# Weight sums of the down projection made from DRAM to DRAM, and two more gate/up pairs by Strassen's scheme, in a two-layer fp32 decoder trunk on one core

## Chip, core, metric

The kernel runs on one core of one Trainium2 chip. The metric is the device time of one execution, in microseconds (us), as a median of several. Where a time is taken from one profiled execution, the text says so.

The engines that matter: TensorE (PE: matmuls, with its weight loads shown as PEld), VectorE (DVE), ScalarE (ACT), GpSimd (POOL) and the 16 DMA engines of the core, which are fed by three queues: one that SyncE (SP) issues, one that ACT issues and one that POOL issues. In the profile these are q1 (SP), q10 (ACT) and q0 (POOL).

## What is computed

Two layers on x of 512 tokens by 1024 features, in fp32. Each layer has a mixer (layer 0: causal pooling; layer 1: causal differential attention), then a SwiGLU feed-forward with 2816 hidden features:

```python
x = layernorm(ALPHA * x + mixer(x))
x = layernorm(ALPHA * x + (silu(x @ w_gate) * (x @ w_up)) @ w_down)
```

The change is in the feed-forward of both layers. Every fp32 product is made of three fast matmuls: each operand is split into a high part (ACT rounds it, a CAST in the profile) and a low part (DVE subtracts the high part), and high·high, high·low and low·high are summed.

## The kernel before

**Weights.** A list `wall` in DRAM holds all weights in blocks of 128x1024 fp32 (512 KB). SP loads blocks in order into five `raw` buffers (`RAWS`, `refill`). ACT and DVE split a block into a pair of parts, six of which fit (`WBUFS`).

**Gate and up products (`ffn`).** The 22 columns of 128 hidden features form 11 pairs; pair k holds columns k and k+11. A pair needs four blocks. An ordinary pair (`plain`, called for each column f) makes four products of 24 matmuls with 512 moving columns. A pair in `SPLIT` (`strassen(k)`) splits the 2x2 block product of {gate, up} x {first, second half of the features} x {first, second 256 tokens} by Strassen's scheme: seven products P1, Q5, P6, Q3, P7, P2, Q4 of 24 matmuls with 256 moving columns. It pays for this with sums: four sums of two weight blocks on DVE (L566, in place in the raw buffers), sums of quarters of x, made once per layer into `xs` (`sums_of_x`: twelve DVE operations of 128x1024 and four ACT casts), and DVE and ACT operations that combine the products (L829 to L849). Before, pairs 4 to 10 are split and pairs 0 to 3 are ordinary. At the start of a layer the first columns (three in layer 0, two in layer 1) are done in halves of 256 tokens, since x arrives late.

**Order.** The program is written out by hand, and each engine keeps its own order. After each product `ahead` issues the splits for later products, so that parts are ready about five products early. An engine goes on as soon as its own queue and semaphores let it; nothing else ties a queue to the place where an instruction stands in the code.

**Down projection.** It uses the same scheme with seven products, over items (p, i): p one of the seven, i one of six groups of rows of `w_down` (`PAIRS`: five of two rows, one of one). Three of the seven take blocks of `wall` as they are; the other four take sums of blocks: with b0 to b3 the four blocks of a group, b0+b1, b1+b3, b0+b1+b3 and b0+b1+b3+b2. Before, they are made during the gate and up products of the same layer, in eleven slices: `load_terms` has POOL issue two loads of 512 KB into free rows of `hid` or into the buffer `gb`, and a third that adds to the first as it lands (`accum_op`); `sum_terms` has DVE make two sums of 128x512 (L671, L672), and then ACT issue two stores to `tsum` in DRAM. The down phase reads `tsum` back through SP (`fetch_item`).

**Affine.** The LayerNorm gain and bias that belong to the residual (`affine(n, s)`: two DVE operations of 128x1024 per 128 tokens, L205 and L206) are done early in each gate phase. The parameters sit in `gb`.

**POOL** also raises the variance to the power -1/2 for each LayerNorm (L177), makes one low part per attention head (`sql`, L110), and issues loads of `ssum` in the down phase (L726).

Of the kernel before, what the change touches and what calls it, by code (L numbers as in the profile page):

```python
# [12 lines left out]
F32 = mybir.dt.float32  # L13
# [3 lines left out]
ALU = mybir.AluOpType  # L17

P = 128
# [3 lines left out]
DEPTH = 2  # L23
# [31 lines left out]
def trunk(ctx, tc, x, wall, pscale, lam_p, subln, table, lng, lnb, band, first, onehot, out):  # L55
# [398 lines left out]

# [8 lines left out]
    def ffn(layer, late):  # L463
# [5 lines left out]
        with tc.tile_pool(name=f"ffn{layer}", bufs=1) as fp:  # L469
# [6 lines left out]


            order = [k + j * HALF for k in range(HALF) for j in range(2)]
            tsum = dram.tile([4, len(PAIRS), P, 1024], F32, name=f"tsum{layer}")
            ssum = dram.tile([P, 2, 2, HALF, 256], F32, name=f"ssum{layer}")  # L480

            def block(i, b):

                if PAIRS[i][1] == 2:
                    return wall[c1 + 4 * i + b]
                return wall[c1 + 20 + b // 2][:, (b % 2) * 512 : (b % 2 + 1) * 512]


            items = [(p, i) for p in DOWN for i in range(len(PAIRS))]
# [4 lines left out]
            def fetch_item(j):  # L494
                p, i = items[j]
                w = 512 * PAIRS[i][1]
                t = keep.tile([P, 1024], F32, tag="raw", name=f"r{layer}_{j}", bufs=RAWS)[:, :w]
                src = {"P1": 0, "P2": 2, "Q3": 3}
                if p in src:
                    nc.sync.dma_start(out=t, in_=block(i, src[p]))  # L500
# [78 lines left out]
            def ahead(upto):  # L579
                advance(upto)  # L580
                if upto > len(chunks):
                    prepare(upto - len(chunks), upto - len(chunks))

            def product(acc, j, lo, hi):
                h, l = halves[j]
                for k in range(KB):
                    mm3(
                        wide(acc, lo, hi),
                        (h[:, k * P : (k + 1) * P], l[:, k * P : (k + 1) * P]),
                        x_at(k, lo, hi),  # L590
                        k == 0,
                        k == KB - 1,
                    )
# [47 lines left out]
                low(3, r3)  # L641
                yield

            terms = {}
            rows_of = hid.rearrange("p (j k) t -> p j k t", j=2)

            def term_slice(k):
                return slice(k % 2 * 512, (k % 2 + 1) * 512)  # L650

            def load_terms(k):
                if k < HALF - 1:
                    c = c1 + 4 * (k // 2)
                    src = wall[c : c + 4][:, :, term_slice(k)].rearrange("(j r) p t -> p j r t", j=2)
                else:
                    src = wall[c1 + 20 : c1 + 22].rearrange("j p (r t) -> p j r t", r=2)
                if k == 1:
                    t = rows_of[:, :, 4:6, :]
                elif k % 2 == 0 and k < HALF - 1:  # L660
                    t = rows_of[:, :, 9:11, :]
                else:
                    t = keep.tile([P, 2, 2, 512], F32, tag="gb", name=f"b{layer}_{k}")
                for j in range(2):
                    nc.gpsimd.dma_start(out=t[:, j], in_=src[:, j])  # L665
                nc.gpsimd.dma_start(out=t[:, 0], in_=src[:, :, 1], accum_op=ALU.add)  # L666
                terms[k] = t

            def sum_terms(k):
                t = terms.pop(k)  # L670
                tt(t[:, 1, 1], t[:, 0, 0], t[:, 1, 1], op=ALU.add)  # L671
                tt(t[:, 1, 0], t[:, 1, 1], t[:, 1, 0], op=ALU.add)  # L672
                yield
                dst = tsum[:, k // 2, :, term_slice(k)].rearrange("(j r) p t -> p j r t", j=2)
                for j in range(2):
                    nc.scalar.dma_start(out=dst[:, j], in_=t[:, j])
                if k + 2 < HALF - 1 and k != 1:
                    load_terms(k + 2)
                if k == HALF - 2:
                    load_terms(HALF - 1)  # L680

            summed_rows = [0]
            behind = []

            def weight_sums():
                g = sum_terms(summed_rows[0])
                summed_rows[0] += 1
                next(g)
                behind.append(g)

            def sum_hidden(k):

# [45 lines left out]
            def prepare(upto, lefts):  # L738
# [11 lines left out]
            load_terms(0)  # L750
            load_terms(1)
            sums = sums_of_x()
            for lo in (0, 256):
                for f in range(early):
                    for i in range(2):
                        product(accs[f][i], 2 * f + i, lo, lo + 256)
                        if not lo and (f, i) in late:
                            late[f, i]()
                        if not lo:
                            advance(2 * early, True)  # L760
                    if lo:
                        advance(2 * f + 6)
                        gated(order[f], *accs[f])
                        affine(n - 1, f)
                        catch_up()
                        if f < 2:
                            weight_sums()
                            next(sums)
                        if f == 1:
                            behind.append(sum_hidden(0))  # L770

            def plain(f):
                k = f // 2
                j = index[k] + 2 * (f % 2)
                a = (bank(f"g{layer}_{f}"), bank(f"u{layer}_{f}"))
                for i in range(2):
                    product(a[i], j + i, 0, S)
                    ahead(j + i + 5)
                    if f >= 3:
                        next(sums, None)  # L780
                    catch_up()
                gated(order[f], *a)
                if f < SB:
                    affine(n - 1, f)
                if f in (3, 5, 7):
                    weight_sums()
                if f == 3:
                    load_terms(3)
                if f % 2:
                    behind.append(sum_hidden(k))  # L790

            def strassen(k):
# [18 lines left out]
                for j, p in enumerate(GATE):  # L811
# [15 lines left out]
                    if p == "P1":  # L827
                        g0 = tile_of(0)
                        nc.scalar.copy(both(g0), acc)  # L829
                    elif p == "Q5":  # L830
                        nc.scalar.copy(second, acc)  # L831
                    elif p == "P6":
                        nc.scalar.copy(first, acc)
                    elif p == "Q3":
                        tt(first, acc, first, op=ALU.subtract)  # L835
                    elif p == "P7":
                        tt(second, second, acc, op=ALU.subtract)
                    elif p == "P2":
                        tt(both(g0), acc, both(g0), op=ALU.add)  # L839
                    else:  # L840
                        g1 = tile_of(1)
                        nc.scalar.activation(both(g1), acc, AF.Silu)
                    ahead(index[k] + j + 6)
                    catch_up()
# [5 lines left out]
                if k < HALF - 1:  # L850
                    weight_sums()
                behind.append(sum_hidden(k))

            f = early
            while f < FB:
                if f // 2 in SPLIT:
                    strassen(f // 2)
                    f += 2
                else:
                    plain(f)  # L860
                    f += 1
            load_gb(n)

            while behind:
# [90 lines left out]
    def attention(late):  # L955
        n = 2
        with tc.tile_pool(name="attn", bufs=1) as ap:
# [225 lines left out]
            for h in range(HEADS):  # L1183
# [35 lines left out]
                ready(where[0] + 3)  # L1219
                if h > 0:  # L1220
                    mix(h - 1)
                start_scores(h)
                score_block(h, 0)
                score_block(h, 1)
# [152 lines left out]
```

## Time and profile before

| | |
|---|---|
| median of 3 runs | 951.18 us (951.01 to 952.31) |
| profiled execution | 951.38 us |
| its span, first to last instruction | 949.6 us |
| mean granted TensorE clock | 0.997 |

The profiled execution lies 0.20 us above the median, and 1.78 us of it are outside the span. The stages, in us from the span's start: pooling mixer to about 44; gate and up of layer 0 to 269, with the Strassen pairs from 127.85; down of layer 0 to 367; attention to about 600; gate and up of layer 1 to 836, with the Strassen pairs from 695.00; down and the last LayerNorm to the end.

How to read the rows: in the chain and the timeline a row has start, duration, engine, line and what it writes from what; "x24" is a number of instructions merged; in brackets stand the idle time ahead of a row and what ended it. In rows by window the columns are the window, its length, then busy time of PE, PEld, DVE, ACT, POOL (number of instructions in brackets), the granted clock, the mean busy share of the 16 DMA engines, and GB/s. Instructions of one engine overlap a little: two sums of 128x1024 take 2.48 together, where one alone takes 1.22. A DMA row gives the size and the median time from issue to landing.

### The profile page before, as it was taken

The page shows a single profiled execution, that of the slowest core. Times are in us where ns is not written, and L with a number is a line of the kernel's source. Part 1 is how long each engine was busy: PE and PEld are TensorE (multiplying, and loading weights), DVE is VectorE, ACT ScalarE, POOL GpSimd, SP SyncE. Part 2 cuts the span into 40 slices and gives each one's busy share as a digit, 9 for nine tenths or more (in the row PEclk, how much of TensorE's full clock was granted, in tenths as well). Part 3 has the DMA queues.
Part 4 walks back from the last instruction along what each step waited for, and adds up shares of the span by engine and source line. Part 5 has one row for each costly group of instructions (what it writes and reads, how often), then busy time and mean ns, then how long its engine had stood idle before and what let it go on. Part 6 is the DMA issues. An engine that isn't in the chain of part 4 may idle for free.

```text
span 949.6 us, 15363 instructions
## 1 busy us (share of the span) xinstructions
PE 934.6 (98%) x5976; PEld 845.9 (89%) x5976; DVE 783.4 (82%) x1149; ACT 489.9 (52%) x788; POOL 108.6 (11%) x133
## 2 busy tenths in 40 slices
PE   9899999999999999999999999999999999999996
PEld 8798899999988888988888888998899999988885
DVE  8858989999988688688777677789779999987678
ACT  6662245555554467665556552833344554564450
POOL 4120211110001200000000000211111110001101
PEclk9999999999999999999999999999999999999998
DMA  9288998976878964323242233396978885878942
GB/s 237 100 261 256 302 290 265 268 237 212 263 249 272 361 221 133 115 89 100 60 141 79 67 89 89 109 319 191 295 254 248 249 269 205 260 247 275 352 175 90
DMA packets 82248, 196.99 MB, mean 207 GB/s; under 512 B 14804, under 2 KB 26324, under 8 KB 82174
## 3 DMA queue, kind: packets, MB, share of 16 engines
q1 hardware_dynamic: 42876, 115.07, 37.1%
q0 software_dynamic: 15520, 46.14, 17.7%
q10 hardware_dynamic: 23778, 34.78, 10.1%
q8 instruction: 47, 0.77, 0.3%
q14 instruction: 27, 0.22, 0.1%
HBM read 159.25 MB, written 36.72 MB: 206 GB/s over the span
## 4 chain that ended last, share of the span: by engine, by line
PE 90%; DVE 6%; ACT 2%; issue 1%; DMA 1%; POOL 0%; DVEq 0%; SPq 0%; POOLq 0%
PE A L820 17%; PE P L886 13%; PE C L820 8%; PE Q L886 6%; PE B L820 4%; PE g L129 3%; PE u L129 3%; PE u L128 3%; PE u L127 3%; PE g L128 3%; PE g L127 3%; PE s L1085 2%; PE v L127 2%; PE v L129 2%; PE v L128 2%; PE q L128 2%
## 5 line engine op out<-in xcount | busy, mean ns | idle before, releaser
L566 DVE TENSOR_TENSOR raw<-raw,raw 128x1024 f32<-128x1024 f32 x56 | 68.3, 1219 | 0.5
L224 ACT ACTIVATE y<-pt,bT,gT 128x128 f32<-128x128 f32 x96 | 36.0, 455 | 22.7 <-PE pt L213 22.7
L109 ACT CAST xs<-hid 128x512 fp32r<-128x512 f32 (+1 forms) x60 | 34.7, 581 | 24.4 <-DVE hid L734 24.4
L110 DVE TENSOR_TENSOR xs<-hid,xs 128x512 fp32r<-128x512 f32 (+1 forms) x60 | 38.4, 642 | 7.8 <-ACT xs L109 7.8
L1095 ACT ACTIVATE p<-p,mn 128x128 f32<-128x128 f32 (+3 forms) x64 | 35.3, 553 | 14.9 <-DVE mn L1090 14.9
L665 POOL DMA_DIRECT2D b<-in_wall x20 | 14.0, 707 | 175.6 <-DMA tsum<-b 92.6
L726 POOL DMA_DIRECT2D xs<-ssum x24 | 17.4, 727 | 141.5 <-PE Q L886 120.3
L598 DVE TENSOR_TENSOR hid<-sg,u 128x512 f32<-128x512 f32 x16 | 11.0, 687 | 26.1 <-PE u L129 14.1
L177 POOL TENSOR_TENSOR rs<-rs,mhalf 128x1 f32<-128x1 f32 x16 | 12.5, 784 | 172.2 <-DVE rs L176 132.8
L110 DVE TENSOR_TENSOR xt<-y,xt 128x512 fp32r<-128x512 f32 x24 | 16.3, 689 | 17.4 <-ACT xt L109 17.4
L665 POOL DMA_DIRECT2D hid<-in_wall x24 | 18.7, 822 | 84.5 <-DMA tsum<-hid 30.7
L1090 DVE CUSTOM_DVE_ANT_0 p<-s,bias 128x128 f32<-128x128 f32 (+3 forms) x64 | 28.1, 485 | 0.0
L110 POOL TENSOR_TENSOR sql<-sq,sqh 128x512 fp32r<-128x512 f32 x7 | 9.1, 1293 | 165.3 <-ACT sqh L109 165.3
L702 ACT CAST v<-u 128x512 fp32r<-128x512 f32 x22 | 13.6, 620 | 26.9 <-DVE u L700 26.7
L168 DVE BATCH_NORM_STATS2 st<-res 128x6 f32<-128x512 f32 x32 | 22.2, 695 | 1.1
L846 ACT ACTIVATE sg<-sg 128x512 f32<-128x512 f32 x14 | 8.9, 633 | 25.7 <-DVE sg L839 25.7
L110 DVE TENSOR_TENSOR heads<-k,heads 128x512 fp32r<-128x512 f32 x8 | 5.5, 693 | 19.9 <-ACT heads L109 19.9
L614 ACT CAST xs<-hid 128x1024 fp32r<-128x1024 f32 x8 | 8.4, 1051 | 24.1 <-DVE hid L631 11.6
L666 POOL DMA_DIRECT2D hid<-in_wall x12 | 14.8, 1232 | 50.1 <-DMA hid<-in_wall 50.1
L1109 DVE SCALAR_TENSOR_TENSOR p<-p,sm,p 128x128 f32<-128x128 f32 (+3 forms) x32 | 17.6, 551 | 1.1
L835 DVE TENSOR_TENSOR hid<-C,hid 128x512 f32<-128x512 f32 x14 | 9.7, 691 | 10.4 <-PE C L820 8.8
L831 ACT COPY hid<-C 128x512 f32<-128x512 f32 x14 | 8.2, 587 | 19.4 <-PE C L820 19.4
(1119 smaller groups left out, 3726.3 us busy)
## 6 DMA issues: line engine op xcount, KB each, us to landing
raw<-in_wall SPq DMA_DIRECT2D x122, 512.0 KB, 4.6
r<-tsum SPq DMA_DIRECT2D x40, 512.0 KB, 4.3
hid<-in_wall POOLq DMA_DIRECT2D x36, 512.0 KB, 7.1
b<-in_wall POOLq DMA_DIRECT2D x30, 512.0 KB, 5.7
r<-in_wall SPq DMA_DIRECT2D x30, 512.0 KB, 4.9
tsum<-hid ACTq DMA_DIRECT2D x24, 512.0 KB, 5.3
ssum<-v ACTq DMA_DIRECT2D x22, 512.0 KB, 4.1
tsum<-b ACTq DMA_DIRECT2D x20, 512.0 KB, 5.1
```

What stands on the lines that cost most here:

```text
L109: nc.scalar.copy(dst_h, src)
L110: (low or nc.vector).tensor_tensor(dst_l, src, dst_h.bitcast(F32), op=ALU.subtract)
L127: nc.tensor.matmul(acc, ah, bh, start=start, stop=False)
L128: nc.tensor.matmul(acc, ah, bl, start=False, stop=False)
L129: nc.tensor.matmul(acc, al, bh, start=False, stop=stop)
L224: nc.scalar.activation(y[:, k, :], pt[:, k * P : (k + 1) * P], AF.Identity, bias=bT[:, n, kk : kk + 1], scale=gT[:, n, kk : kk + 1],)
L566: tt(t, raws[pair[0]], raws[pair[1]], op=ALU.add)
L665: nc.gpsimd.dma_start(out=t[:, j], in_=src[:, j])
L820: nc.tensor.matmul(o, w[:, c], x[:, kk, :], start=p in ("P1", "Q5", "P2") and f + kk + e == 0, stop=p in ("Q4", "Q3", "P2") and (f, kk, e) ...
L886: nc.tensor.matmul(accs[s], x[:, k, r], y[:, c], start=first and k == 0 and e == 0, stop=last and k == m - 1 and e == 2, skip_group_check= ...
L1090: nc.vector.tensor_tensor_reduce(out=p, in0=accs[c][:, :w], in1=biases[h][:, w - 1 :: -1] if w < S else biases[h][:, ::-1], op0=ALU.add, o ...
L1095: nc.scalar.activation(p, p, AF.Exp, bias=mn[:, q, c : c + 1], scale=-1.0, accum_out=sm[:, q, c : c + 1],)
```

## The change

- The four sums of down-weight blocks are made from DRAM to DRAM, with no buffer in SBUF and nothing on DVE or ACT: for each, six copies of block or earlier sum into `sums[layer][q][i]`, then six DMAs that add another block to it as they land. All 48 per layer are issued by POOL, with at most 8192 B per descriptor row. `load_terms`, `sum_terms`, `weight_sums` and `tsum` go.
- The code takes these steps from a generator: for layer 0, `pace()` after each gate or up product takes 0.69 step on average; for layer 1, six steps stand in each of the eight attention heads.
- `SPLIT` gains pairs 2 and 3, in both layers. The layout of `wall` follows.
- `sums_of_x` starts as soon as x is complete and is done before pair 2.
- The affine operations move from the first columns to the Strassen pairs 3 to 10: one DVE operation at each Q3 (`affines`).

```diff
-SPLIT = (4, 5, 6, 7, 8, 9, 10)
+SPLIT = (2, 3, 4, 5, 6, 7, 8, 9, 10)
...
+    sums = [
+        [
+            [
+                dram.tile([P, 512 * m], F32, name=f"t{layer}_{q}_{i}")
+                for i, (_, m) in enumerate(PAIRS)
+            ]
+            for q in range(4)
+        ]
+        for layer in range(DEPTH)
+    ]
...
+    def sum_steps(layer, c):
+
+        made = sums[layer]
+        for q, start, b in ((0, None, 1), (1, None, 3), (3, 0, 3), (2, 3, 2)):
+            for adds in range(2):
+                for i in range(len(PAIRS)):
+                    if adds:
+                        source, op = block(c, i, b), dict(accum_op=ALU.add)
+                    else:
+                        source, op = made[start][i] if start is not None else block(c, i, q), {}
+                    nc.gpsimd.dma_start(
+                        out=made[q][i], in_=source, max_dma_last_dim=8192, **op
+                    )
+                    yield
...
                 else:
                     m = {"Q5": 0, "P6": 3, "P7": 1, "Q4": 2}[p]
-                    nc.sync.dma_start(out=t, in_=tsum[m, i, :, :w])
+                    nc.sync.dma_start(out=t, in_=sums[layer][m][i])
...
-            def load_terms(k):
...
-                for j in range(2):
-                    nc.gpsimd.dma_start(out=t[:, j], in_=src[:, j])
-                nc.gpsimd.dma_start(out=t[:, 0], in_=src[:, :, 1], accum_op=ALU.add)
-                terms[k] = t
-
-            def sum_terms(k):
-                t = terms.pop(k)
-                tt(t[:, 1, 1], t[:, 0, 0], t[:, 1, 1], op=ALU.add)
-                tt(t[:, 1, 0], t[:, 1, 1], t[:, 1, 0], op=ALU.add)
-                yield
...
-                for j in range(2):
-                    nc.scalar.dma_start(out=dst[:, j], in_=t[:, j])
...
+            def affines():
+                for s in range(SB):
+                    for j, op in enumerate((ALU.mult, ALU.add)):
+                        tt(res[:, s, :], res[:, s, :], gbs[n - 1][:, j, :], op=op)
+                        yield
...
+            xsums, scaling = sums_of_x(), affines()
+            turned_at = 2 * max(late)[0] + max(late)[1]
+            paced = [0.0]
+
+            def pace():
+
+                if not layer:
+                    paced[0] += 0.69
+                    while paced[0] >= 1:
+                        next(terms[0], None)
+                        paced[0] -= 1
...
                         product(accs[f][i], 2 * f + i, lo, lo + 256)
+                        pace()
                         if not lo:
                             advance(2 * early, True)
+                            for _ in range({1: 2, 2: 1}.get(2 * f + i - turned_at, 0)):
+                                next(xsums)
                     if lo:
                         advance(2 * f + 6)
                         gated(order[f], *accs[f])
-                        affine(n - 1, f)
+                        next(xsums)
                         catch_up()
-                        if f < 2:
-                            weight_sums()
-                            next(sums)
...
+                    pace()
                     ahead(index[k] + j + 6)
+                    next(xsums, None)
+                    if p == "Q3" and k > 2:
+                        next(scaling, None)
...
-                if k < HALF - 1:
-                    weight_sums()
...
+                for _ in range(3):
+                    next(terms[1], None)
                 query(accs[0], w[0], 256 if h == 0 else 0, 512)
```

What this does to the order on the engines, at the three places on which the prediction rests. A row has the line, the operation, output and inputs, the shape, and in brackets the semaphores that it waits for: a DMASW is a landing of a POOL DMA, a DMAHW one of an SP or ACT DMA. Lines below 440 are the same in both; later ones move: L566 becomes L597, L572 L603, L611 L642, L598 L629, L835 and the rows behind it L830 and on.

POOL at the start of the gate phase of layer 0, before:

```order
L445 MEMSET line 8x128
L665 DMA hid_529<-in_wall 128x2x512 [waits DMAHW2_49,DMAHW4_49,DMAHW0_49,DMAHW6_49,PE_49,DMAHW7_49,Activation_49,Pool_49]
L665 DMA hid_529<-in_wall 128x2x512
L666 DMA hid_529<-in_wall 128x2x512 [waits DMASW0_49]
L665 DMA hid_529<-in_wall 128x2x512 x2
L666 DMA hid_529<-in_wall 128x2x512 [waits DMASW3_49]
L665 DMA hid_529<-in_wall 128x2x512 [waits DMAHW7_49,DMASW2_49,DVE_49]
L665 DMA hid_529<-in_wall 128x2x512 [waits DMAHW0_49,DMASW1_49,DVE_49]
L666 DMA hid_529<-in_wall 128x2x512 [waits DMASW6_49]
L665 DMA b_3_1031<-in_wall 128x2x512 [waits DMAHW3_49,DMAHW2_49,DVE_49]
```

The same place after the change:

```order
L445 MEMSET line 8x128
L484 DMA t_0_0_526<-in_wall 64x2048
L484 DMA t_0_1_527<-in_wall 64x2048
L484 DMA t_0_2_528<-in_wall 64x2048
L484 DMA t_0_3_529<-in_wall 64x2048
L484 DMA t_0_4_530<-in_wall 64x2048
L484 DMA t_0_5_531<-in_wall 128x512
L484 DMA t_0_0_526<-in_wall 64x2048 [waits DMASW0_49]
L484 DMA t_0_1_527<-in_wall 64x2048 [waits DMASW1_49]
L484 DMA t_0_2_528<-in_wall 64x2048 [waits DMASW2_49]
L484 DMA t_0_3_529<-in_wall 64x2048 [waits DMASW3_49]
```

Before, the loads wait for DVE and for stores (the buffers must come free); after, the first six wait for nothing and the others for landings of POOL's own DMAs alone; so it goes on through all 48 rows, with no other POOL instruction between them. In layer 1 a `sql` of an attention head stands behind each six.

DVE where x is complete in layer 0, before:

```order
L110 TENSOR_TENSOR xt<-y_3_1_670,xt 128x4x128
L598 TENSOR_TENSOR hid_529<-sg_0_797,u_0_534 128x512
L205 TENSOR_TENSOR res<-res,gb_522 128x1024
L206 TENSOR_TENSOR res<-res,gb_522 128x1024
L671 TENSOR_TENSOR hid_529<-hid_529 128x512
L672 TENSOR_TENSOR hid_529<-hid_529 128x512
L611 TENSOR_TENSOR hid_529<-xt 128x1024
L572 TENSOR_TENSOR g_6l<-raw_503,g_6h 128x1024
```

and after:

```order
L110 TENSOR_TENSOR xt<-y_3_1_712,xt 128x4x128
L642 TENSOR_TENSOR hid_577<-xt 128x1024 x4
L629 TENSOR_TENSOR hid_577<-sg_0_847,u_0_581 128x512
L657 TENSOR_TENSOR hid_577<-hid_577 128x1024
L659 TENSOR_TENSOR hid_577<-hid_577 128x1024
L603 TENSOR_TENSOR g_6l<-raw_503,g_6h 128x1024
L603 TENSOR_TENSOR g_7l<-raw_510,g_7h 128x1024
L629 TENSOR_TENSOR hid_577<-sg_11_918,u_1_583 128x512
L662 TENSOR_TENSOR hid_577<-hid_577 128x1024
```

Four sums of x now stand ahead of the first gated column, and affine and weight sums are gone from behind it.

DVE in a steady Strassen pair (the second half of pair 6), before:

```order
L837 TENSOR_TENSOR hid_529<-hid_529,A_6_1823 128x2x256
L566 TENSOR_TENSOR raw_1684<-raw_1684,raw_1852 128x1024
L572 TENSOR_TENSOR g_40l<-raw_1852,g_40h 128x1024
L572 TENSOR_TENSOR g_39l<-raw_1684,g_39h 128x1024
L839 TENSOR_TENSOR sg_6_0_1850<-B_6_1825,sg_6_0_1850 128x512
L566 TENSOR_TENSOR raw_1684<-raw_1684,raw_1891 128x1024
L572 TENSOR_TENSOR g_41l<-raw_1756,g_41h 128x1024
L848 TENSOR_TENSOR hid_529<-sg_6_0_1850,hid_529 128x2x256
L849 TENSOR_TENSOR hid_529<-sg_6_1_2048,hid_529 128x2x256
L671 TENSOR_TENSOR b_7_1617<-b_7_1617 128x512
L672 TENSOR_TENSOR b_7_1617<-b_7_1617 128x512
L572 TENSOR_TENSOR g_42l<-raw_1891,g_42h 128x1024
```

and after:

```order
L737 TENSOR_TENSOR res<-res,gb_522 128x1024
L832 TENSOR_TENSOR hid_577<-hid_577,A_6_2026 128x2x256
L597 TENSOR_TENSOR raw_1886<-raw_1886,raw_2056 128x1024
L603 TENSOR_TENSOR g_46l<-raw_2056,g_46h 128x1024
L603 TENSOR_TENSOR g_45l<-raw_1886,g_45h 128x1024
L834 TENSOR_TENSOR sg_6_0_2053<-B_6_2028,sg_6_0_2053 128x512
L597 TENSOR_TENSOR raw_1886<-raw_1886,raw_2091 128x1024
L603 TENSOR_TENSOR g_47l<-raw_1960,g_47h 128x1024
L847 TENSOR_TENSOR hid_577<-sg_6_0_2053,hid_577 128x2x256
L848 TENSOR_TENSOR hid_577<-sg_6_1_2252,hid_577 128x2x256
L603 TENSOR_TENSOR g_48l<-raw_2091,g_48h 128x1024
```

One operation of 128x1024 on the residual has come in ahead of L832, and two of 128x512 have gone behind L848.

More of the change, by code (lines that the diff above doesn't have):

```diff
@@ L453, in trunk, with block @@
     base = [2]
+    sums = [
[8 more added lines that the diff above has]
+    ]
+    def block(c, i, b):
+        if PAIRS[i][1] == 2:
+            return wall[c + 4 * i + b]
+        return wall[c + 20 + b // 2][:, (b % 2) * 512 : (b % 2 + 1) * 512]
+    def sum_steps(layer, c):
[11 more added lines that the diff above has]
+                    yield
+    terms = [
+        sum_steps(layer, base[0] + 2 * FB if layer == 0 else total - FB) for layer in range(DEPTH)
+    ]
     ROWS = [slice(k, k + n) for k, n in PAIRS]
@@ L478, in ffn @@
             order = [k + j * HALF for k in range(HALF) for j in range(2)]
-            tsum = dram.tile([4, len(PAIRS), P, 1024], F32, name=f"tsum{layer}")
             ssum = dram.tile([P, 2, 2, HALF, 256], F32, name=f"ssum{layer}")
[L482 to L486, printed above, removed]
             items = [(p, i) for p in DOWN for i in range(len(PAIRS))]
@@ L499, in fetch_item @@
                 if p in src:
-                    nc.sync.dma_start(out=t, in_=block(i, src[p]))
+                    nc.sync.dma_start(out=t, in_=block(c1, i, src[p]))
                 else:
                     m = {"Q5": 0, "P6": 3, "P7": 1, "Q4": 2}[p]
-                    nc.sync.dma_start(out=t, in_=tsum[m, i, :, :w])
+                    nc.sync.dma_start(out=t, in_=sums[layer][m][i])
                 drops[j] = t
@@ L842, in strassen @@
                         nc.scalar.activation(both(g1), acc, AF.Silu)
+                    pace()
                     ahead(index[k] + j + 6)
+                    next(xsums, None)
+                    if p == "Q3" and k > 2:
+                        next(scaling, None)
                     catch_up()
@@ L861, in ffn @@
                     f += 1
+            for _ in scaling:
+                pass
             load_gb(n)
@@ L1221, in attention @@
                     mix(h - 1)
+                for _ in range(3):
+                    next(terms[1], None)
                 start_scores(h)
```

37 lines of the change are left out of this document (removed).

## The prediction, as it was made before the changed kernel ran

> **What bounds the kernel now.** I read the busy times first, then the stages by window, then the chain and the timelines of PE and DVE inside the gate phases, and last the DMA queues. The page:
>
> ```profile
> span 949.6 us, 15363 instructions
> ...
> PE 934.6 (98%) x5976; PEld 845.9 (89%) x5976; DVE 783.4 (82%) x1149; ACT 489.9 (52%) x788; POOL 108.6 (11%) x133
> ```
>
> PE is idle for 15.0 us in all. By window:
>
> ```profile
> 44.00:73.30 29.30, 29.30 (x247) 29.30 (x247) 17.70 (x19) 18.09 (x31) 7.25 (x10) 1.00 0.85 261
> 73.30:127.90 54.60, 54.60 (x243) 45.24 (x243) 48.13 (x56) 17.82 (x21) 8.11 (x9) 1.00 0.84 269
> 127.90:269.00 141.10, 141.10 (x1177) 141.09 (x1176) 132.61 (x161) 73.24 (x95) 14.41 (x16) 1.00 0.82 258
> 380.00:560.00 180.00, 179.84 (x1178) 159.18 (x1178) 135.26 (x314) 106.81 (x239) 10.05 (x11) 1.00 0.30 92
> 629.50:695.00 65.50, 65.50 (x292) 54.27 (x291) 53.53 (x62) 21.10 (x25) 10.79 (x12) 1.00 0.84 259
> ```
>
> In the gate phases PE never pauses, at the full granted clock; DVE is next with 94% of the Strassen stage (132.61 of 141.10), and the DMA engines are busy for 0.82 to 0.85, against 0.30 in attention. So PE work that goes is time that goes, as long as DVE and the DMAs stay behind their cover.
>
> **The price of a pair on PE.** Ordinary products run from the first to the second of these rows in layer 0, and from the third to the fourth in layer 1; Strassen products from the second to the last:
>
> ```profile
> 73.26 0.40 PE L127 MATMUL g<-xt,g_6h 128*128 128x512 f32 x1
> ```
> ```profile
> 127.85 2.87 PE A L820 x24
> ...
> 173.92 2.88 PE A L820 x24
> ...
> 268.96 14.99 PE P L886 x66
> ...
> 695.00 2.87 PE A L820 x24
> ```
> ```profile
> 629.53 0.40 PE L127 MATMUL g<-xt,g_4h 128*128 128x512 f32 x1
> ```
>
> Ten products in 54.59 us and twelve in 65.47: 5.457 each, 227 ns per matmul of 512 columns. Forty-nine products in 141.11: 2.880 each, 120 ns per matmul of 256. A pair costs 4 x 5.457 = 21.83 as it was and 7 x 2.880 = 20.16 by Strassen. Four pairs save 4 x 1.67 = **6.7 us**. That is little, because a matmul of half the columns costs 0.53 of the whole. The Trainium skill (TensorE: Matmul & The Clock Gate, Back-to-back issue gap) gives 518 and 262 cycles; by it a pair would save 2.4 us and four 9.5. No row here shows that ratio, so the sum goes by the rows.
>
> **DVE.** A steady pair before (pairs 5 and 6):
>
> ```profile
> 149.83 1.22 DVE L572 TENSOR_TENSOR g_27l<-raw,g_27h 128x1024 fp32r<-128x1024 f32 x1
> ...
> 152.17 0.68 DVE L671 TENSOR_TENSOR b<-b 128x512 f32<-128x512 f32 x1
> 152.89 0.69 DVE L672 TENSOR_TENSOR b<-b 128x512 f32<-128x512 f32 x1
> 153.50 1.22 DVE L572 TENSOR_TENSOR g_28l<-raw,g_28h 128x1024 fp32r<-128x1024 f32 x1
> ...
> 159.63 0.69 DVE L835 TENSOR_TENSOR hid<-C,hid 128x512 f32<-128x512 f32 x1 [0.45 <-PE C L820]
> 160.24 2.48 DVE L566 TENSOR_TENSOR raw<-raw,raw 128x1024 f32<-128x1024 f32 x2
> ...
> 166.75 1.23 DVE L572 TENSOR_TENSOR g_32l<-raw,g_32h 128x1024 fp32r<-128x1024 f32 x1
> ...
> 179.79 0.69 DVE L835 TENSOR_TENSOR hid<-C,hid 128x512 f32<-128x512 f32 x1 [0.81 <-PE C L820]
> ```
>
> From L835 to L835 it is 20.16 us, of which DVE waits 0.81 for PE: it fills 19.35. The weight sums take 1.33 of that (152.17 to 153.50) and go; an affine step of 128x1024 comes for pairs 3 to 10, 1.14 to 1.25. So DVE fills 19.2 or so, still under 20.16. DVE also stays ahead of PE: g_32l is done at 167.98 and PE begins with it at 173.92, 5.9 us later. Affine, weight sums and ACT's stores therefore cost or gain nothing in themselves. If that cover went, each us of DVE per pair would cost 9 us per layer.
>
> Over the kernel DVE loses 44 sums of 128x512 and gains, for each new pair, four sums, three combinations and one split less. ACT has half its time free.
>
> **Pair 2 earlier.** In layer 0 it starts where column 4 started, 73.26 + 2 x 5.46 = 84.2. The sums of x must be ready for Q5 at 87.1 and P6 at 89.9. DVE's free stretch there:
>
> ```profile
> 62.09 0.69 DVE L598 TENSOR_TENSOR hid<-sg,u 128x512 f32<-128x512 f32 x1 [6.55 <-PE u L129]
> ```
>
> The four sums that now stand ahead of this row take about 4.6 us and fit into its 6.55. Going on row by row through the new order, at 1.14 per 128x1024 and 0.6 per 128x512, I get the first low part of `xs` at 71, the last at 86, g_10l (for P6) at 84 and g_12l (for the fifth product, 95.7) at 89.5: six us to spare, if the blocks are there. Layer 1 has two ordinary columns before pair 2 and more room. Cost: nothing, bounded by 0 and some 2 us.
>
> **The sums by DMA.** Volume per layer: 24 copies and 24 adds, 11.5 MB each. The queues:
>
> ```profile
> q1 hardware_dynamic: 42876, 115.07, 37.1%
> q0 software_dynamic: 15520, 46.14, 17.7%
> q10 hardware_dynamic: 23778, 34.78, 10.1%
> ```
>
> Over 16 engines and 949.6 us, SP's queue moved 20.4 GB/s per engine while it moved, ACT's 22.7. POOL's 46.1 MB are 44 copies, 22 adds and 24 loads of `ssum`; with copies at 20.4, 11.6 GB/s is left for the adds. So the new sums fill all engines for (11.5/20.4 + 11.5/11.6)/16, or 97 us per layer; the old ones, with half as many adds and with stores, 98. That the destination is DRAM is not in the trace: ACT's stores to DRAM bound it below (no dearer), twice the add above. I take the row's rates.
>
> In layer 1 the 97 us lie in 180 us of attention where the engines are busy for 0.30, and the gate phase loses them. POOL's own work there is one `sql` per head, and it has long idle stretches ahead of each:
>
> ```profile
> POOL sql L110 <- ACT sqh L109: 165.3, 7, 37.9
> ```
>
> ```profile
> L665 POOL DMA_DIRECT2D hid<-in_wall x24 | 18.7, 822 | 84.5 <-DMA tsum<-hid 30.7
> L666 POOL DMA_DIRECT2D hid<-in_wall x12 | 14.8, 1232 | 50.1 <-DMA hid<-in_wall 50.1
> ```
>
> Six issues of 0.8 to 1.2 us fit into that, and what they wait for was issued a head earlier. Cost: nothing; with the cover gone, a late `sql` would reach PE a head later.
>
> In layer 0 the order shows no wait for compute, so `pace()` paces nothing: POOL starts all 48 right behind this row, eight in flight.
>
> ```profile
> 44.04 0.20 POOL L445 MEMSET line<- 8x128 f32 x1
> ```
>
> They share the engines with SP's weight blocks until, by my estimate, 130 to 190 us; after that the queue is freer than before. What a block can bear: the buffer that g_27l frees is refilled at
>
> ```profile
> 151.11 0.33 SPq L99 DMA_DIRECT2D raw<-in_wall  x1
> ```
>
> and read by the second sum of 160.24, at 161.4: 10.3 us. Landing times of blocks, from 75 to 130 us and in attention, and of the adding DMAs:
>
> ```profile
> DMA to landing us min/median/max: 5.6/6.2/7.5
> ```
> ```profile
> DMA to landing us min/median/max: 3.4/3.5/5.0
> ```
> ```profile
> DMA to landing us min/median/max: 5.8/6.9/11.3
> ```
>
> With DMA at 0.84 no block took over 7.5. There are 2.8 us left to the reader, then 5.9 to PE. The old traffic came in bursts of three with waits between; the new is steady. Cost bounded by 0 and the slow rival below; nearest are the rows from 75 to 130 us, so I take 0.
>
> **Sum.** Span 949.6 - 6.7 = 942.9, with the 1.8 outside 944.7; the median stands 0.2 under the profiled execution: **944.5 us**. 0.2% is about what the measurement can tell from no change, 1.9 us.
>
> **Rivals.**
>
> 1. *Blocks a little late in layer 0.* DVE slips below its cover for some pairs and PE waits 2 to 4 us: 946 to 949. For it: POOL's queue is never empty. Against: the 2.8 and 5.9 us above.
> 2. *The gain is eaten.* If the engines take a packet from each queue in turn, a block is eight rows of 4 KB per engine at 0.2 us, each behind an 8 KB row at 0.40 (copy) or 0.70 (add): 8 x 0.75 = 6.0 us per block, where a pair needs four in 20.16, one per 5.04. From 44 to 84 SP needs the engines for five blocks and two loads of `gb`, some 12 us, so 69 of the 97 us of sums remain at 84, stretched by 0.75/0.55 to 94: 4.7 pairs, each 3.9 us late, 18 in all. The cover is 2.8 + 5.9 and 0.9 of DVE's for each pair, some 12: 6 us lost, 951.
> 3. *Slower.* The same turn-taking with rows a third dearer, as DRAM destinations may be: 6.8 us per block, 7 us per pair over 4.2 pairs, 29 less 12, 17 lost: 962. It decides once a block takes over 5.04 us for four pairs. The Trainium skill states such turns (DMA: Bandwidth & Descriptors, Queues, rings and completion order). Against both 2 and 3 speaks the window in which the queues were busiest, where packets overlapped (share 1.05) instead of taking turns, and PE lost nothing:
>
> ```profile
> 105.00:120.00 15.00, 15.00 (x68) 12.41 (x67) 13.87 (x18) 5.74 (x8) 2.70 (x3) 1.00 1.05 352
> ```
>
> 4. *More than the sum.* A matmul of 256 columns at half of 227 ns would make a pair cost 19.1, and four would save 10.8: 940.4. Every Strassen product in the chain shows 120 ns instead. The skill's ratio of 262 to 518 is nearly this case.
>
> **How the numbers follow.** All hidden 0.48 (own range 943 to 946); rival 1 0.15; rival 2 0.13; rival 3 0.20; rival 4 0.04. Faster by over 0.2% are the first, 1 and 4: 0.67; within: 0.13; slower: 0.20. That is below the simple reading of the sum, since the trace shows no DMA from DRAM to DRAM at all. The range 942.5 to 956 leaves out rival 4 and most of 3, a fifth in all.
>
> **What will show it.** Strassen in the chain: 18 pairs at 20.16 us from about 84 and 651 us on, without a gap. POOL's 48 DMAs of layer 0 bunched from 44 us, not spread to 265. Block landings in that stretch under 10 us; DVE idle before a weight sum, released by a DMA, would speak for 1 to 3, and gaps of PE between 95 and 190 us for 2 or 3. DMA share in the gate phase of layer 1 down to about 0.4, up in attention to 0.7 or 0.8. I am wrong if the DRAM sums are dear per row or if SP's blocks lose their turns.

## The result, and the profile after

| | before | after |
|---|---|---|
| median (lowest to highest), us | 951.18 (950.64 to 952.31), 5 runs | 960.1 (959.34 to 961.13), 5 runs |
| after over before, 95% interval | | 1.0093 (1.0081 to 1.0104) |
| profiled execution: time, span, us | 951.38, 949.6 | 959.34, 957.5 |

The changed kernel is 8.9 us slower; 944.5 was forecast, with 956 as the upper end. The profile page of after first: TensorE, the DMA strip (40 slices of 23.9 us), the queues, and VectorE's weight sums.

```profile
PE 934.3 (98%) x6264; PEld 857.4 (90%) x6264; DVE 793.8 (83%) x1145; ACT 506.3 (53%) x812; POOL 112.4 (12%) x163
...
DMA  9299999433467974857898863133343344478952
...
q1 hardware_dynamic: 42876, 115.07, 36.8%
q0 software_dynamic: 11264, 57.68, 22.4%
q10 hardware_dynamic: 11810, 11.71, 3.5%
...
L597 DVE TENSOR_TENSOR raw<-raw,raw 128x1024 f32<-128x1024 f32 x72 | 87.8, 1220 | 3.8 <-DMA raw<-in_wall 3.2
```

Counted from 0, layer 0's gate phase lies in slices 2 to 11: the DMA engines are full to the end of slice 6, some 167 us, and at 0.3 to 0.4 behind it, until the down projection's loads come. In layer 1's gate phase (26 to 34) they are down to 0.3 to 0.4, as forecast. For the first time a weight sum waits for a DMA (the last row). But TensorE's total of busy time says nothing of the loss. The loss is seen when the span is cut at the same matmuls of each kernel: from the timeline, TensorE's first product over all columns in layer 0 (`g` of column 3), the first product of each down projection, and the first product of layer 1's gate phase. The third kernel is the experiment `e3_both`, below, where both causes are gone.

| stretch, us | before | after | `e3_both` |
|---|---|---|---|
| start to column 3 of layer 0 | 73.26 | 72.61 | 73.63 |
| column 3 to the down projection, layer 0 | 195.54 | 203.60 | 193.66 |
| down projection and attention | 336.75 | 336.76 | 336.73 |
| gate phase, layer 1 | 230.41 | 231.44 | 227.20 |
| the rest | 113.64 | 113.09 | 113.68 |

So 8.1 us were lost in layer 0 and 1.0 in layer 1, where 3.3 each should have been gained; attention took the sums of layer 1 at no cost. Now the chain of after in layer 1, where no sums run beside it (start, length, what; the short pieces left out). It begins with P1 of pair 2.

```profile
658.89 2.87 PE A L815 x24
661.77 2.88 PE C L815 x24
...
676.17 5.76 PE A L815 x48
681.93 2.88 PE C L815 x24
684.81 2.88 PE A L815 x24
687.69 2.89 PE C L815 x24
...
691.28 1.23 DVE raw L597
692.53 1.23 DVE raw L597
693.76 1.14 DVE g_23l L603
694.89 1.13 DVE res L737
696.03 0.61 DVE hid L832
...
696.68 6.01 PE A L815 x48
...
717.45 6.01 PE A L815 x48
```

A bank is the part of TensorE's result memory in which a product is summed: A serves P1, P6, P7 and Q4, C serves Q5 and Q3, B serves P2. A row of 48 on bank A is Q4 of one pair and P1 of the next. Pair 2 is clean. From pair 3 on the chain leaves TensorE behind Q3 and comes back over VectorE: two weight sums, a low part, the affine step (L737), and L832, the subtraction that reads P7's bank A. Q4 writes that bank and waits. The period is 696.68 to 717.45, 20.77 us in place of 20.16; of the 0.61 us, 0.25 are Q4's slower start (6.01 for 5.76), the rest the wait. Pairs 3 to 9 pay, in both layers: 14 x 0.61 = 8.5 us.

Layer 0 in after has the same rows, and three blocks of weights in the chain, each an operand of the two sums for the next pair that VectorE takes in order ahead of L832. VectorE waits 3.0 us for the first of them, in its second sum, 0.2 for the third, and for the second not at all:

```profile
91.72 10.19 DMA raw<-in_wall
...
111.43 11.14 DMA raw<-in_wall
...
128.28 6.01 PE A L815 x48
...
155.46 10.29 DMA raw<-in_wall
```

TensorE's row in the timeline behind the first of them (Q4 of pair 2; the idle time ahead of it in brackets), and SP's blocks from issue to landing, 84 to 130 us:

```profile
105.02 0.80 PE L815 MATMUL A<-xt,g_14h 128*128 128x256 f32 x2 [3.43 <-DVE hid L832]
```

```profile
DMA to landing us min/median/max: 10.2/13.5/17.2
```

And the stretches around that wait; the value behind POOL's is the granted clock:

```profile
98.00:102.00 4.00, 3.58 (x30) 3.38 (x29) 0.99 (x1) 1.06 (x2) 0.50 (x1) 1.00 1.02 269
102.00:106.00 4.00, 0.98 (x4) 0.98 (x5) 4.00 (x4) 2.08 (x2) 0.00 (x0) 0.74 1.05 363
106.00:110.00 4.00, 4.00 (x21) 4.00 (x20) 3.96 (x5) 1.68 (x2) 0.80 (x1) 0.50 1.03 419
110.00:114.00 4.00, 4.00 (x33) 4.00 (x32) 4.00 (x6) 2.09 (x3) 1.56 (x2) 0.91 1.01 416
```

The block issued at 91.72 reaches VectorE's sum at 102; TensorE stands for 3.4 us, and then works at half clock until about 110.7: 21 matmuls in 4 us, 33 in the next 4.

### The profile page after: what moved, and what is told of

Read it like the earlier page. It is cut to its first block, busy times and chain, and to the rows that moved or that the text cites. A ratio compares the mean times of both kernels' runs of the same rounds, so it can differ in the third digit from the quotient of the medians.

```text
span 957.5 us, 15885 instructions
## 1 busy us (share of the span) xinstructions
PE 934.3 (98%) x6264; PEld 857.4 (90%) x6264; DVE 793.8 (83%) x1145; ACT 506.3 (53%) x812; POOL 112.4 (12%) x163
## 3 DMA queue, kind: packets, MB, share of 16 engines
q0 software_dynamic: 11264, 57.68, 22.4%
## 4 chain that ended last, share of the span: by engine, by line
PE 73%; DVE 16%; DMA 4%; ACT 3%; issue 3%; DVEq 0%; POOL 0%; ACTq 0%; SPq 0%; POOLq 0%
PE A L815 15%; PE P L885 13%; PE C L815 9%; PE Q L885 6%; DVE raw L597 4%; DMA raw<-in_wall 3%; PE s L1084 2%; PE v L127 2%; DVE res L737 2%; PE v L128 2%; PE v L129 2%; PE q L128 2%; PE q L129 1%; PE q L127 1%; PE k L127 1%
## 5 line engine op out<-in xcount | busy, mean ns | idle before, releaser
L597 DVE TENSOR_TENSOR raw<-raw,raw 128x1024 f32<-128x1024 f32 x72 | 87.8, 1220 | 3.8 <-DMA raw<-in_wall 3.2
L484 POOL DMA_DIRECT2D t<-in_wall x72 | 51.3, 837 | 53.4 <-DMA t<-in_wall 32.8
L830 DVE TENSOR_TENSOR hid<-C,hid 128x512 f32<-128x512 f32 x18 | 12.5, 692 | 25.2 <-PE C L815 25.2
L845 ACT ACTIVATE sg<-sg 128x512 f32<-128x512 f32 x18 | 11.4, 632 | 35.7 <-DVE sg L834 35.7
L826 ACT COPY hid<-C 128x512 f32<-128x512 f32 x18 | 10.6, 587 | 21.5 <-PE C L815 21.5
L737 DVE TENSOR_TENSOR res<-res,gb 128x1024 f32<-128x1024 f32 x16 | 19.5, 1218 | 0.0
L109 ACT CAST heads<-k 128x512 fp32r<-128x512 f32 x8 | 4.7, 588 | 26.2 <-PE k L129 26.2
L828 ACT COPY hid<-A 128x512 f32<-128x512 f32 x18 | 10.6, 588 | 14.0 <-PE A L815 14.0
L1084 PE MATMUL s<-heads 64*128 64x256 f32 (+2 forms) x192 | 17.9, 330 | 0.0
```

What stands on the lines that cost most here:

```text
L109: nc.scalar.copy(dst_h, src)
L484: nc.gpsimd.dma_start(out=made[q][i], in_=source, max_dma_last_dim=8192, **op)
L597: tt(t, raws[pair[0]], raws[pair[1]], op=ALU.add)
L737: tt(res[:, s, :], res[:, s, :], gbs[n - 1][:, j, :], op=op)
L1084: nc.tensor.matmul(accs[c][:, :wide], a[r, qs], b[r, :wide], start=i == 0, stop=i == 2)
```

## Experiments

Theory A: the burst of layer 0's DMAs makes SP's blocks late. Theory B: the affine step's place costs 0.61 us per pair. The rivals stand in the expectations. Times are medians; "before" ran again beside each group, at 951.1 to 951.3.

**e1_affine_p6: another place for the affine step.**

```diff
-                    if p == "Q3" and k > 2:
+                    if p == "P6" and k > 2:
```

> The changed kernel with one word of it different: the affine step of each pair is issued behind P6 instead of behind Q3, where VectorE stands idle for 1.6 us before it may read Q3's bank. Theory B (the affine step's place costs 0.61 us in each of 14 pairs, since it stands ahead of the subtraction that frees Q4's bank): 960.1 - 8.5 = 951.6 us, pairs of layer 1 at 20.16 instead of 20.77. Rival: VectorE is full, so that the place does not matter: 960 us and pairs at 20.77.

951.27 us (949.47 to 952.93, 11 runs; the profile is of the fastest), 0.9999 of before (0.9991 to 1.0008): 8.8 us won by one name. Where VectorE now runs the step and when bank A comes free (timeline of VectorE, layer 1):

```profile
722.58 1.22 DVE L737 TENSOR_TENSOR res<-res,gb 128x1024 f32<-128x1024 f32 x1
723.72 0.68 DVE L690 TENSOR_TENSOR v<-u,v 128x512 fp32r<-128x512 f32 x1
725.41 0.69 DVE L830 TENSOR_TENSOR hid<-C,hid 128x512 f32<-128x512 f32 x1 [1.01 <-PE C L815]
726.01 2.48 DVE L597 TENSOR_TENSOR raw<-raw,raw 128x1024 f32<-128x1024 f32 x2
728.40 1.22 DVE L603 TENSOR_TENSOR g_37l<-raw,g_37h 128x1024 fp32r<-128x1024 f32 x1
729.54 0.68 DVE L832 TENSOR_TENSOR hid<-hid,A 128x512 f32<-128x512 f32 x1
```

Between Q3's end and Q4, which starts at 731.06, TensorE has P7 and P2, 5.76 us; the work from L830 to L832 fills 4.8 of them, and L832 ends 0.8 to 0.9 us ahead of Q4. A step put there holds up what follows by 1.14 (it takes 1.22, and the next operation starts 0.08 before its end; the two sums do not overlap and take 2.48). That is 0.2 to 0.3 too long, and the stall adds its 0.25 of slow start: 0.6 with the signals between. Layer 1's gate phase is 227.2 us now. B holds.

**e10_double: twice the step in half the pairs** (on `e6_two`, below).

```diff
-                    if p == "P6" and k > 2:
+                    if p == "Q3" and 2 < k < 7:
                         next(scaling, None)
+                        next(scaling, None)
```

> Layer 0's sums written block by block, and the affine steps back behind Q3, but two of them in each of four pairs (3 to 6) instead of one in each of eight. If the cost of a place is what the step takes over VectorE's slack there (0.61 us for one step, so 0.61 + 1.14 = 1.75 for two): pairs 3 to 6 take 21.9 us, the others 20.16, and 946.1 + 8 x 1.75 = 960 us. Rival: each place costs a fixed 0.61 whatever is put there: 951.

960.73 us, 1.0100 of before (1.0085 to 1.0115). The chain in layer 1:

```profile
674.75 5.76 PE A L816 x48
...
693.47 1.15 DVE res L738
694.64 1.23 DVE res L738
...
696.52 6.02 PE A L816 x48
...
718.55 6.02 PE A L816 x48
...
740.58 6.02 PE A L816 x48
```

(Rows move by a line between these kernels: L816 and L738 are the L815 and L737 of after.) Pairs of 22.03 us (718.55 less 696.52) against 21.9 expected; from pair 8 on they are at 20.16. A place costs what stands in it over the slack there.

**e2_plain_l0 and e3_both: no sums of layer 0** (the down projection of layer 0 reads plain weight blocks in their place), e2 with the affine steps behind Q3, e3 with them behind P6.

```diff
 def pace():
-                if not layer:
-                    ...
+                return
 ...
-                    nc.sync.dma_start(out=t, in_=sums[layer][m][i])
+                    nc.sync.dma_start(out=t, in_=sums[1][m][i] if layer else block(c1, i, m))
```

> The changed kernel without the 48 DMAs of layer 0's weight sums; the down projection of layer 0 reads plain weight blocks of the same size where it read the sums, so its output is not the reference's. Theory A (the burst of these DMAs makes SP's blocks late, some 7 us in all): 953 us, weight blocks of layer 0's gate phase landing in 3.5 to 4 us. Rival: what layer 0 lost was lost to the earlier Strassen pairs or to VectorE's order: 959 to 960 us.

> Both edits: affine steps behind P6, no sums of layer 0 (output not the reference's). If the two losses are separate and all there is: 960.1 - 8.5 - 7.1 = 944.5 us, which is the forecast by the PE sum alone. Rival (the same stalls were counted twice, or something else is late next): 946 to 949.

e2 954.91 us (ratio 1.0039, 1.0027 to 1.0052), e3 946.82 (0.9952, 0.9939 to 0.9964), in the range of e3's rival. A costs 5.2 us beside the affine steps, not 7, and 4.5 without them; the two losses nearly add: 8.8 and 5.2 for the 13.3 between after and e3. 2.3 us to the forecast are left, of which layer 0 holds 1.5 (193.66 against 195.54 - 3.34). There pair 2 is late, by VectorE and ScalarE alone (waits of e3, 60 to 110 us; its L811, L828 and L824 are after's L815, L832 and L828):

```profile
PE A L811 <- DVE hid L828: 0.5, 1, 0.5
PE A L811 <- ACT hid L824: 0.3, 1, 0.3
```

With the slow starts behind them (P7 takes 2.97 us instead of 2.88, Q4 and P1 6.02 instead of 5.76) that is 1.1 of the 1.5.

**e8_plain_pairs: what the two more Strassen pairs per layer gain.** e3 with

```diff
-SPLIT = (2, 3, 4, 5, 6, 7, 8, 9, 10)
+SPLIT = (4, 5, 6, 7, 8, 9, 10)
```

> Affine steps behind P6 and no sums of layer 0 (output not the reference's), with pairs 2 and 3 of both layers by plain products again: seven Strassen pairs of eleven as in the kernel before. By the prediction's term (1.67 us for each of four pairs, less 1.3 that pair 2 of layer 0 waits in its profile): 946.8 + 6.7 - 1.3 = 952.2 us. By rival 4 (2.7 us a pair): 956. If the Strassen pairs gained nothing: 947.

951.08 us, 0.9999 of before (0.9990 to 1.0008). The four pairs gain 4.3 us in the medians and 5.1 by the table's stretches (1.88 and 3.21; e8 has 195.54 and 230.41, to the hundredth those of before); the start and the end, which scatter by about 1 us between kernels, are 1.1 us longer in the profile of e3. Rival 4 is out. By such differences layer 0 of after is 195.54, less 1.88 for the two pairs, with 4.28 for the affine steps (e2's 197.94 against e3's 193.66) and 5.66 for the burst (203.60 against 197.94).

**e4_paced and e11_paced_again: a real pace.** Affine steps behind P6, and ahead of each DMA of layer 0's sums

```diff
                     while paced[0] >= 1:
+                        o = paced[1] % 48
+                        nc.scalar.copy(flag[:, o : o + 1], eps_t[:, :1])
+                        nc.gpsimd.tensor_copy(sink[:, o : o + 1], flag[:, o : o + 1])
                         next(terms[0], None)
...
```

> Affine steps behind P6, and each DMA of layer 0's sums made to wait: ScalarE copies one column into a flag at its place in the program, GpSimd reads that flag before it issues the DMA. One DMA per 4.2 us from 50 to about 265 us instead of a backlog of eight. If the backlog is what makes blocks late: 944.5 to 946.5 us, blocks landing within 7 us. Rival (the bytes cost the time, spread or not; each block loses a turn to the copy in flight): 949 to 953 us.

948.66 us (945.82 to 950.04, 10 runs), 0.9973 (0.9963 to 0.9982), between the two expectations: 2.6 better than the burst, 1.8 behind no sums, and the runs scatter (the profile is of the fastest). The DMAs are issued from 50.97 to 249.30 us; blocks land in 4.9 us (median, 84 to 130 us), at most 8.6.

> The paced kernel once more, for a profile of one of its slower runs (its ten runs went from 945.8 to 950.0 us, and the profiled one was the fastest). If slower runs come from a block that is late enough to stop TensorE for about 3 us, after which the granted clock is 0.50 for some 6 us (as behind the 3.4 us gap of the changed kernel): a gap of that size between 84 and 200 us, a stretch of half clock right behind it, mean clock 0.995. If they come from elsewhere (the start, attention, layer 1): no such gap in layer 0's gate phase.

947.55 us, one run. No gap of 3 us and no half clock, but a gap at the known place: 1.6 us, where the profile of e4 has 0.5. The same block stands ahead of it in all of these kernels, an operand of pair 3's second sum, in front of Q4 of pair 2. Chain and wait, of e4, e5 (below), e11 and e1 in this order:

```profile
92.00 7.27 DMA raw<-in_wall
```
```profile
92.48 7.36 DMA raw<-in_wall
```
```profile
92.63 8.39 DMA raw<-in_wall
```
```profile
91.78 10.23 DMA raw<-in_wall
```
```profile
PE A L820 <- DVE hid L837: 0.5, 1, 0.5
```
```profile
PE A L815 <- DVE hid L832: 0.6, 1, 0.6
```
```profile
PE A L820 <- DVE hid L837: 1.6, 1, 1.6
```
```profile
PE A L815 <- DVE hid L832: 3.5, 1, 3.5
```

Each gap is the block's time less 6.8 us; so it is in after (10.19 and 3.4) and in e7, below (8.23 and 1.5). In e3, e6 and e9, where blocks land sooner, this block is not in the chain and the gap is 0.4 to 0.5 by VectorE's own work. So up to some 7.2 us this block costs nothing. The whole cost of A in layer 0 of e1's profile follows: its gap is 3.0 us above e3's 0.5, and Q4 with the next P1, 48 matmuls, take 7.27 instead of 6.02 us at the lowered clock: 4.3 us, as much as e1's layer 0 is longer than e3's (197.95 against 193.66). What makes the runs of e1 and e4 scatter was not profiled for the slowest ones; with what follows from the two e4 profiles, this block's landing is the candidate. The mean granted clocks on record fit it, without showing it: four runs of e4 with 0.995 took 948.7 to 950.0 us, the six with 0.997 or 0.998 took 945.8 to 948.9; in e1 the slowest run has 0.992 and the fastest 0.996.

**e5_rows_2k, e6_two, e9_two_2k: what makes a block late.** Layer 0's sums in rows of 2 KB (e5), block by block (e6), both (e9); affine steps behind P6.

```diff
-                        out=made[q][i], in_=source, max_dma_last_dim=8192, **op
+                        out=made[q][i], in_=source, max_dma_last_dim=8192 if layer else 2048, **op
```

```diff
-            for adds in range(2):
-                for i in range(len(PAIRS)):
-                    if adds:
+            n = len(PAIRS)
+            for adds, i in [(a, i) for a in range(2) for i in range(n)] if layer else [(a, i) for i in range(n) for a in range(2)]:
+                if True:
+                    if adds:
```

> The changed kernel with the affine steps behind P6, and the 48 DMAs of layer 0's sums cut into rows of 2 KB instead of 8 KB; still a backlog. If an engine takes rows of the two queues in turn (rivals 2 and 3 of the prediction), a block of SP waits for four times less: landings of 4 to 7 us instead of 13 to 15, and 947 to 948 us instead of 951.3. If a block waits for the bytes that stand ahead of it, whatever their rows: landings of 13 to 15 us as before, 951 us.

> The same, rows of 8 KB, but layer 0's sums written block by block: copy, add, next copy, so that each add waits for the copy just ahead of it and at most two of these DMAs are in flight instead of eight. If a block waits for the bytes ahead of it: 1 MB at 340 GB/s is 3 us instead of 12, landings of 5 to 7 us, 947 to 948 us. If rows taken in turn make the landing (a row of 8 KB is always there): landings stay at 13 to 15 and the time at 951.

> Affine steps behind P6, layer 0's sums written block by block (two in flight) and in rows of 2 KB. If row size and number in flight both lengthen a block's wait (13.4 us with eight of 8 KB, 7.2 with eight of 2 KB, 5.5 with two of 8 KB, in the stretch from 84 to 130 us), a block lands in 4 to 5 us here; if only the bytes ahead counted, 5.5. The time is 946 us in both cases, since no landing over some 8 us is left to hold TensorE up.

e5 946.27 us (0.9947, 0.9934 to 0.9960), e6 946.13 (0.9944, 0.9930 to 0.9958), e9 945.76 (0.9945, 0.9933 to 0.9958). Each alone removes A, and all three beat both kernels by about 5 and 14 us, with the full work done. Landings of SP's blocks from 84 to 130 us, e1, e5, e6, e9 and, without sums, e3:

```profile
DMA to landing us min/median/max: 10.2/13.4/16.7
```
```profile
DMA to landing us min/median/max: 6.8/7.2/9.7
```
```profile
DMA to landing us min/median/max: 4.4/5.5/9.1
```
```profile
DMA to landing us min/median/max: 3.6/4.7/6.8
```
```profile
DMA to landing us min/median/max: 3.5/3.9/4.3
```

Above the 3.9 of e3 stand 9.5 us with up to eight DMAs of 8 KB rows in flight, 3.3 with eight of 2 KB, 1.6 with two of 8 KB, 0.8 with two of 2 KB. Neither expectation holds alone. Row size counts by itself: the engines are as busy in e5 as in e1 (1.07 and 1.03 from 84 to 130 us). The order by blocks does two things at once: fewer DMAs are in flight, and POOL, which waits for landings, issues its last one at 244 us instead of 147, so that the engines are busy for 0.88. Which of the two shortens the landing is not separated. How the engines choose among what is queued is not settled.

**e7_copies: the adds as copies** (layer 0's sums then hold one block each, not a sum).

```diff
-                        source, op = block(c, i, b), dict(accum_op=ALU.add)
+                        source, op = block(c, i, b), dict(accum_op=ALU.add) if layer else {}
```

> Affine steps behind P6, and layer 0's 24 adding DMAs made plain copies of the same blocks (output not the reference's); still eight in flight. If the adds are the dear half (11.6 against 20.4 GB/s per engine, as the prediction worked out), the burst shrinks from about 120 to 75 us, blocks land in 8 to 11 us, and the time is 948 to 949. If copies from DRAM to DRAM are as dear as adds: burst and time as with the adds, 951.

947.77 us (0.9962, 0.9949 to 0.9975); the burst is issued within 84 us instead of 103 (less of a cut than expected), blocks land in 11.3 us (median, 84 to 130), the tight one in 8.23. By the queue's share POOL's DMAs take 191 us of all engines (20.2% of 945.1) where e1 has 212 (22.4% of 947.7) and e3, without layer 0's sums, 128 (13.5% of 944.9). So layer 0's sums cost 85 us where the prediction worked out 97, and an add 21 us more than a copy per 11.5 MB where it had 27.

## Why the prediction was wrong, point by point

- *The Strassen term* (6.7 us): right in mechanism, a little mis-sized. Products take 2.88 us and a pair 20.16 wherever nothing stops it; layer 1 gained 3.21 of 3.34. The remainder comes from a reading: the first row of the ordinary stretch is from the timeline and the last from the chain, which has the same matmul 0.16 us later (127.85 against 127.68). From the timeline alone a product costs 5.44, a pair saves 1.61 and two save 3.22. "Pair 2 earlier, six us to spare, cost 0 to 2": it was 1.3 in layer 0 (3.21 - 1.88), and the text had taken 0.
- *The step on VectorE failed first.* The prediction put the affine step at nothing. It compared VectorE's total per pair, 19.2 us, with 20.16 and found room. The total was right: VectorE fits even in e1. But the room lies ahead of L830, where VectorE waits for Q3 to end, and the step was put behind it, into the 5.76 us that had 0.9 to spare before Q4 needs bank A. The cover it named, 5.9 us from g_32l to the matmul that reads it, was that of a weight's low part, not that of the bank. The order rows shown ahead of the prediction have L737 right in front of L832; nothing asked what L832 releases. Cost 8.5 us by the periods, 8.8 by e1.
- *The cover of a block failed second.* The prediction put the burst at nothing, too. What a block can bear, 10.3 us from issue and 5.9 more, was read in a steady pair of before, at 151 us. The tight block is the one at 92 us, in pair 2, new as a Strassen pair: 6.8 us and nothing behind it, as VectorE is full there (its rows in after leave no gap from 83 us to this wait).
- *The landings.* Taken: under 7.5 us as in the busiest window of before, where loads came in bursts of three. With eight in flight: 13.5.
- *Rivals.* 2 had the size (6 us lost to DMA; 5.2 by e2) but not the way: it spread a slip over 4.7 pairs, by 6.0 us per block, and it was one gap of 3.4 us with a stretch of half clock behind it. 3 came nearest to the time (962), but its 17 us by DMA are not what happened, and its working does not come out: rows a third dearer would be 0.73 us on average for 0.55 and make a block 7.5 us, not 6.8. The Trainium skill (DMA: Bandwidth & Descriptors, Queues, rings and completion order) has queues served in turn, by packets of some 9 to 17 descriptors; no run here shows the size of a turn, which rivals 2 and 3 took as one row. e5 agrees that the row matters, from 13.4 to 7.2 us. e6, with rows of 8 KB and 5.5 us, shows that the row is not all; it does not decide against turns, since its engines were less busy.
- *Right:* `pace()` paces nothing (POOL's first issue at 43.55, the last at 148.74 us); layer 1's sums are hidden in attention (336.7 to 336.8 us in all columns of the table); the price per byte, nearly (85 us for 97).
- *The sum.* 944.5 was the time with both losses gone; e3 has 946.8, e9 945.8.

## What to carry to other kernels

An operation that fits into an engine's total may still be late: for each place, look up which buffer the next instruction on that engine releases, and how long before its need it now does so. The room is where the engine is shown waiting, and moving the step there cost nothing here (e8, with the steps behind P6, has the gate phases of before). For bulk copies that run beside loads with a deadline, limit what is in flight by dependences (copy, then its add) or cut the rows, and take the deadline from the tightest consumer, not from a steady one.

## What was not expected of the hardware

- A gap of 3.4 us on TensorE was followed by a granted clock of 0.50 for 6.8 us in all in after (2.1, 4.0 and 0.7 us by the clocks of its three rows from 102 to 114 us), and a gap of 3.5 us by 3.4 us of it in e1; gaps of 0.5 to 1.6 us by none. The rows of e1 beside those of after, above:

```profile
102.00:106.00 4.00, 0.88 (x4) 0.88 (x5) 3.89 (x4) 2.09 (x2) 0.00 (x0) 0.82 1.04 398
106.00:110.00 4.00, 4.00 (x28) 4.00 (x28) 3.96 (x5) 1.82 (x3) 1.42 (x2) 0.75 1.03 419
```

  The gap alone is not the cost: in after it is 23.26 us from Q4 of pair 2 to Q4 of pair 3 (105.02 above to 128.28 in the chain) instead of 20.77, 2.5 more; in e1 it was 1.25 more. The Trainium skill (TensorE: Matmul & The Clock Gate, Part 1: The HAM clock gate) puts the half rate behind an idle window of about 3.4 us that runs free of the program. The two stretches agree with such a window, as two lengths and one of it. The fall does not quite: by the same rows the clock drops 2.3 us into the gap in after (103.9, the gap from 101.6) and 2.9 us into that of e1, so less than 3.4 us of idle time was enough. Why one of two nearly equal gaps cost twice the other is not shown by a run; a window that runs free of the program would do it.
- A burst of DMAs from DRAM to DRAM, up to eight in flight, made a 512 KB load of another queue take 13.5 us (after) instead of 3.9 (e3).
